# Experts as blocks in program order with a fifth row buffer, and a front that fetches no early rows during the z gates

## The chip, the core and the metric

The kernel runs on one core of one Trainium2 chip. The metric is the device time of one execution in microseconds (us); below is better. The engines are TensorE (PE, its weight loads PEld), VectorE (DVE), ScalarE (ACT), GpSimd (POOL) and SyncE (SP), which issues most of the DMAs. Each engine executes its instructions in the order in which they stand in its queue.

## What is computed

One decoder layer over 1024 tokens of width 1024, all float32, in eight tiles of 128 tokens. First the mixing part (cut here to a line), then product-key retrieval of single-neuron experts ("PEER"), then a last RMSNorm:

```python
x = x + gate_m * (concat(pool_mixer, ssd_mixer(z, x, B, C, dt)) @ w_out)   # after rmsnorm, modulate, h @ w_in
h = modulate(rmsnorm(x, norm_ffn), shift_f, scale_f)
q = (h @ w_query)                      # 8 heads x 2 halves of 128
v1, i1 = top_k(q[:, :, 0] @ keys1, 16); v2, i2 = top_k(q[:, :, 1] @ keys2, 16)
top_s, pos = top_k(v1[..., None] + v2[..., None, :], 16)      # of 16 x 16 pairs
idx, gates = i1 * 128 + i2 at pos, softmax(top_s)             # 128 experts of 16384 for a token
act = gelu(sum_d(h * expert_down[idx]))
x = x + gate_f * sum_k(gates * act * expert_up[idx])
out = rmsnorm(x, norm_final)
```

## The kernel before

**Front.** `front(gi)` (line 390 on) runs three times, over the token tiles 0-1, 2-4 and 5-7. In each: blocks of the input projection with convolution, the SSD chunks, the z gates (`product` with `w_z`, line 522), the output projection (`product` with `w_o`, line 542), the second norm, and the query projection with the scores and the first top 16 (lines 567 to 609). What a tile's experts are is worked out by `select` (line 732). It is a generator: pieces of it are put between the blocks of the next group by `drain(rate)`, with a priority as if they stood 2000 instructions later.

**Two ways for the experts.** Tiles 1 to 4 ("dense", `DT`) go through all 16384 experts on PE: `select` turns their choices into one-hot matmuls and stores a dense gate table `gd` in HBM (lines 812 to 848). Tiles 0, 5, 6, 7 ("gathered", `GT`) fetch the 128 expert rows of each token by indirect DMA on POOL and work on DVE. Tile 0 is done in the front by `ahead` (line 858), two half rows of 4 KB a token in a step, 129 steps; `fetch(n)` takes n of these steps after each block of the front (`FETCH` has n by group, 1.6 in the second and 0.5 in the third). Tiles 5 to 7 are done by `gather` (line 888) beside the dense experts: 128 steps each, a whole row of 8 KB a token (down and up). One step is an indirect DMA into one of four row buffers (three, and one more in the experts' part), a dot product on DVE (line 910), Gelu and gate on ACT (911, 912) and, one step later, the weighted sum on DVE (903), which frees the buffer. Tiles 6 and 7 have their top 16 of scores put off into this part too (`selects`, line 708).

**Dense experts.** `experts` (line 954) goes over 128 blocks of 128 experts. For each: load `raw` (the block's down weights), split it into a rounded part `dnh` (ACT, 1023) and a rest `dnl` (DVE, 1024), 24 matmuls of a faster fp32 format into `m` (1033), Gelu on ACT (1036), times the gates on DVE (1037). For each unit of three blocks, `mm2` (line 993) does 48 matmuls into eight outputs (1007): four stay in PSUM (`res`), four pass through two rotating banks (`rot`) and are added to `ys` in SBUF by DVE (1014). After the last unit each dense tile gets `finish` (line 925).

**What sets the order.** The whole program is laid out at compile time by a scheduler that simulates it and gives each engine the ready instruction of highest priority. The gather steps of the experts' part are drained behind each block (`steps * b // (NK - SB * LEAD)`, line 1042) at the late priority, so where they land between PE's blocks is the scheduler's choice. The memory of the front's pools is used again by the experts' pools; a tile there waits for the last reader of what lay under it.

Of the kernel before, what the change touches and what calls it, by code (L numbers as in the profile page):

```python
# [17 lines left out]
D = 1024  # L18
# [26 lines left out]
LEAD = 2  # L45
# [3 lines left out]
MORE = 1  # L49
# [13 lines left out]
FETCH = (0, 1.6, 0.5)  # L63


class Trunk:
    def __init__(self, ctx, tc, I, out):
        self.ctx, self.tc, self.nc, self.I, self.out = ctx, tc, tc.nc, I, out
        self.bg = []
        self.due, self.owed, self.few = 0, 0, 2  # L70
        self.early, self.taken = None, 0

# [30 lines left out]


    def consts(self):
# [9 lines left out]
        self.rooms = {name: self.pool(name) for name in ("rz", "rx", "rp", "r1")}  # L115
# [182 lines left out]
    def product(self, n, w, kps, a, rate, then=None):  # L298

        for q in range(4):  # L300
            acc = [self.psa.tile([128, 512], FT, name="acc") for _ in range((n + 1) // 2)]
            acc = [acc[i // 2][:, i % 2 * 256:i % 2 * 256 + 256] for i in range(n)]
            for kp in kps:
# [9 lines left out]
                self.fetch(self.frate)  # L313
# [71 lines left out]
    def front(self, gi):  # L385
# [136 lines left out]
        for q, acc in self.product(n, I["w_z"], (0, 1), lambda k, c: h[:, k, c], RATEZ[gi]):  # L522
# [46 lines left out]
        for b in range(16):  # L569
# [33 lines left out]
            for i in range(n):  # L603
# [4 lines left out]
                scr = self.tp.tile([128, 128], FT, name="tscr", bufs=2)  # L608
# [99 lines left out]
    def selects(self, lp):  # L708

        for t, v, pi in self.late:  # L710
            for h in range(0, 8, 2):
                sc = lp.tile([128, 4, 128], FT, name="sc")
                self.nc.sync.dma_start(sc, self.scd[LATE.index(t), :, 2 * h:2 * h + 4])
                for b in range(4):
                    scr = self.tp.tile([128, 128], FT, name="tscr", bufs=2)
                    self.top16(sc[:, b], v[:, h + b // 2, b % 2], pi[:, h + b // 2, b % 2], scr)
                    if b % 2:
                        yield
# [15 lines left out]
    def select(self, t, v, pi):  # L734
# [15 lines left out]
        key = tp.tile([128, 8, 2, 16], BF, name="key")  # L750
        nc.vector.tensor_copy(key, pi)
# [3 lines left out]
        for h in range(8):  # L755
            scr = tp.tile([128, 128], FT, name="tscr", bufs=2)
# [15 lines left out]
        for start, length in ROWS:  # L772
            nc.vector.tensor_scalar(q, p, float(start), float(length - (start == SINGLE)), op0=OP.is_ge, op1=OP.mult)
            nc.vector.tensor_tensor(r2, r2, q, op=OP.subtract)
            if start < SINGLE:
                nc.vector.tensor_scalar(q, p, float(start), None, op0=OP.is_ge)
                nc.vector.tensor_tensor(r1, r1, q, op=OP.add)  # L777
        yield
        idx = tp.tile([128, 2, 8, 16], FT, name="idx")
        for j, r in enumerate((r1, r2)):  # L780
            for h in (0, 4):
# [4 lines left out]
                nc.vector.tensor_tensor(oh, oh, key[:, hs, j].unsqueeze(3).to_broadcast([128, 4, 16, 16]), op=OP.mult)  # L786
# [101 lines left out]
    def gather(self, j):  # L888
# [3 lines left out]
        h2 = gp.tile([128, D], FT, name="h2", bufs=1)  # L892
        nc.sync.dma_start(h2, self.h2r[j * 128:(j + 1) * 128, :])
# [11 lines left out]
        for s in range(128):  # L905
# [9 lines left out]
            prev = (u, a, s)  # L915
            yield
        add(*prev)
# [5 lines left out]
        self.finish(t, [acc[:, :512], acc[:, 512:]], rows, self.residual(xx[:, :D], t), xx[:, D:])  # L923
        yield

# [215 lines left out]
```

## Time and profile before

| | |
|---|---|
| runs | 2895.31, 2899.98, 2903.27 us; median 2899.98 |
| the profiled execution | 2912.44 us, span 2910.6 us, mean granted clock 0.948 |
| busy | PE 91%, DVE 82%, ACT 29%, POOL 30% of the span |
| moved | 893.31 MB, mean 307 GB/s |

The page gives shares of the whole span, which has three parts with different limits: the front (0 to about 1221 us), the dense experts with the gather (to about 2811 us) and what follows PE's last full stretch (to 2910.6 us). A digit in a slice line is a busy share in tenths; PEclk is TensorE's granted clock in tenths of full speed.

### The profile page before, as it was taken

How to read it: one execution, taken by the hardware profiler on the slowest of the kernel's cores; microseconds unless marked ns; L12 is line 12 of the kernel's file. 1: busy time of each engine (PE TensorE's matmuls, PEld its weight loads, DVE VectorE, ACT ScalarE, POOL GpSimd, SP SyncE). 2: the span in 40 equal slices, each digit the busy share in tenths (PEclk: the TensorE clock that was granted, in tenths of full speed). 3: DMA queues.
4: the chain of work that ended last, by engine and by line, in shares of the span. 5: the costliest groups of instructions: out<-in, count | busy, mean ns of one | idle time of the engine just before them, and what ended most of it. 6: DMA issues, size and time to landing. Idle time of an engine off the chain costs nothing. (4 is left out here: it accounts for less than half of the span.)

```text
span 2910.6 us, 31644 instructions
## 1 busy us (share of the span) xinstructions
PE 2663.1 (91%) x10243; PEld 1746.7 (60%) x10244; DVE 2375.6 (82%) x5156; ACT 830.1 (29%) x2244; POOL 884.6 (30%) x679
## 2 busy tenths in 40 slices
PE   8899986789889989699999999999999999999961
PEld 5688555676557876465655666666666666666630
DVE  6625898979999879899999777787877777778887
ACT  3523451322254342322222222222222222222211
POOL 0000066554440005022333333333333333333343
PEclk9999987899989989899999999999999999999985
DMA  8655389999863679888999999899999989998986
GB/s 304 222 172 173 103 296 331 356 362 361 289 234 124 185 220 383 277 310 323 352 354 356 356 366 337 336 364 361 346 348 351 370 320 372 348 368 339 356 320 234
DMA packets 264278, 893.31 MB, mean 307 GB/s; under 512 B 25904, under 2 KB 110000, under 8 KB 212656
## 3 DMA queue, kind: packets, MB, share of 16 engines
q0 software_dynamic: 92448, 541.11, 49.0%
q1 hardware_dynamic: 171664, 350.18, 34.7%
q8 instruction: 81, 1.33, 0.2%
q14 instruction: 85, 0.70, 0.1%
HBM read 840.86 MB, written 50.34 MB: 306 GB/s over the span
## 5 line engine op out<-in xcount | busy, mean ns | idle before, releaser
L907 POOL DMA_INDIRECT row<-in_ud,eidx x384 | 547.5, 1426 | 1105.8 <-DVE yacc L903 870.4
L903 DVE SCALAR_TENSOR_TENSOR yacc<-row,act,yacc 128x1024 f32<-128x1024 f32 x381 | 488.5, 1282 | 67.9 <-ACT act L912 65.1
L910 DVE SCALAR_TENSOR_TENSOR row<-row,h 128x1024 f32<-128x1024 f32 x384 | 467.1, 1218 | 51.1 <-DMA row<-in_ud,eidx 50.8
L1007 PE MATMUL rot<-up,w 128*128 128x512 f32 x1024 | 464.5, 596 | 4.8 <-DVE ys L1014 4.8
L1007 PE MATMUL res<-up,w 128*128 128x512 f32 x1024 | 458.6, 592 | 0.0
L870 POOL DMA_INDIRECT row<-in_ud,eidx x256 | 313.6, 1225 | 417.3 <-DVE rkb L777 102.1
L911 ACT ACTIVATE act<-act 128x1 f32<-128x1 f32 x384 | 77.1, 201 | 976.0 <-DVE row L910 975.6
L1007 PEld LDWEIGHTS rot<-up,w 128*128 128x128 f32 x1024 | 194.9, 191 | 221.8 <-issue 208.3
L1007 PEld LDWEIGHTS res<-up,w 128*128 128x128 f32 x1024 | 193.8, 189 | 200.5 <-issue 189.4
L1033 PE MATMUL m<-h2h,dnh 128*128 128x512 f32 x1024 | 292.9, 427 | 18.9 <-ACT dnh L1023 18.9
L1033 PE MATMUL m<-h2l,dnh 128*128 128x512 f32 x1024 | 285.6, 413 | 0.0
L1033 PE MATMUL m<-h2h,dnl 128*128 128x512 f32 x1024 | 279.6, 412 | 0.0
L1033 PEld LDWEIGHTS m<-h2h,dnh 128*128 128x128 f32 x1024 | 193.5, 189 | 96.8 <-issue 39.5
L307 PE MATMUL acc<-wraw,r 128*128 128x256 f32 x1024 | 239.3, 388 | 8.3 <-ACT s L525 8.3
L435 PE MATMUL acc<-r,wraw 128*128 128x384 f32 (+1 forms) x768 | 235.0, 464 | 2.3 <-ACT s L439 1.3
L581 PE MATMUL acc<-rz,wraw 128*128 128x384 f32 (+1 forms) x768 | 235.3, 457 | 0.0
L1033 PEld LDWEIGHTS m<-h2l,dnh 128*128 128x128 f32 x1024 | 192.6, 188 | 66.5 <-issue 30.4
L1033 PEld LDWEIGHTS m<-h2h,dnl 128*128 128x128 f32 x1024 | 193.4, 189 | 59.2 <-issue 19.1
L307 PEld LDWEIGHTS acc<-wraw,r 128*128 128x128 f32 x1024 | 196.3, 195 | 37.9 <-ACT s L525 9.9
L1014 DVE TENSOR_TENSOR ys<-rot,ys 128x512 f32<-128x512 f32 x168 | 115.4, 687 | 112.1 <-PE rot L1007 111.6
L435 PEld LDWEIGHTS acc<-r,wraw 128*128 128x128 f32 x768 | 147.7, 195 | 81.8 <-issue 8.6
L581 PEld LDWEIGHTS acc<-rz,wraw 128*128 128x128 f32 x768 | 143.7, 194 | 64.0 <-issue 2.3
(298 smaller groups left out, 3271.3 us busy)
## 6 DMA issues: line engine op xcount, KB each, us to landing
up<-in_ud SPq DMA_DIRECT2D x128, 512.0 KB, 7.4
raw<-in_downT SPq DMA_DIRECT2D x128, 512.0 KB, 7.9
gd<-stage SPq DMA_DIRECT2D x32, 1024.0 KB, 9.3
gates<-gd SPq DMA_DIRECT2D x16, 2048.0 KB, 12.3
wraw<-in_w_c SPq DMA_DIRECT2D x48, 512.0 KB, 5.6
wraw<-in_w_q SPq DMA_DIRECT2D x48, 512.0 KB, 6.3
wraw<-in_w_o SPq DMA_DIRECT2D x36, 512.0 KB, 5.2
row<-in_w_ada SPq DMA_DIRECT2D x32, 512.0 KB, 5.3
```

The source lines that it names most:

```text
L307: self.nc.tensor.matmul(acc[i], a(4 * kp + j, slice(i * 128, (i + 1) * 128)), ws[:, j * 256:(j + 1) * 256], start=kp == kps[0] and j == 0 ...
L435: nc.tensor.matmul(acc[:, :T], wc[:, k * 128:(k + 1) * 128], h[:, k], start=k == 0, stop=k == KB - 1)
L581: nc.tensor.matmul(acc[:, :T], wq[:, k * 128:(k + 1) * 128], g[:, k], start=k == 0, stop=k == KB - 1)
L870: nc.gpsimd.indirect_dma_start(out=u[:, i * D:(i + 1) * D], out_offset=None, in_=src, in_offset=bass.IndirectOffsetOnAxis(ap=e[:, s + i:s ...
L903: nc.vector.scalar_tensor_tensor(acc, u[:, D:], a, acc, op0=OP.mult, op1=OP.add)
L907: nc.gpsimd.indirect_dma_start(out=u, out_offset=None, in_=self.I["ud"], in_offset=bass.IndirectOffsetOnAxis(ap=e[:, s:s + 1], axis=0))
L910: nc.vector.scalar_tensor_tensor(u[:, :D], u[:, :D], 1.0, h2, op0=OP.mult, op1=OP.mult, accum_out=a)
L911: nc.scalar.activation(a, a, AF.Gelu)
L1007: nc.tensor.matmul(ps, w[:, ts], up[:, hs], start=st, stop=sp, skip_group_check=True)
L1014: nc.vector.tensor_tensor(ysum[o], ps, ysum[o], op=OP.add)
L1033: nc.tensor.matmul(p1, dn[x][:, k * 128:(k + 1) * 128], h2[y][:, k], start=(k == 0 and n == 0), stop=(k == KB - 1 and n == 2))
```

## The change

1. **Order.** After the early work is drained, everything that `experts` issues on PE, DVE and ACT keeps the order of the program (`in_order` adds an ordering edge between neighbours on an engine). SP and POOL are left to the scheduler.
2. **The loop is written as a pipeline.** `raw` is loaded three blocks ahead, `dnh` made two ahead, `dnl` one ahead; the gates of a block are applied one block later; the 48 matmuls of a unit are spread over the three blocks of the next one; the adds to `ys` come one block later. The gather steps are paced: 384 steps over blocks 4 to 125, at most five a block.
3. **Five row buffers** in place of four (`MORE = 2`); a tile's `h2` is loaded before the tile ahead of it is finished.
4. **Memory.** The experts' pools are put in another order (`raw` first, `ys` and `gates` late; `up` has 6 buffers, not 7, `w` 6, not 4), and the front's rooms too, so that other tiles lie under them.
5. **Late top 16.** Scores come in single loads of 64 KB two ahead, not four at a time; one `tscr` buffer; the steps of it go with the gather of the tile before, one for eight gather steps.
6. **`select`.** The keys are kept twice side by side, so that the product with the one-hots reads pairs; one fused instruction in place of two, seven times.
7. **Front.** `FETCH` is 1.7 and 0.9 in the second and third group, and none is taken during the z gates.

```diff
-LEAD = 2
+FIRST, LAST = 4, 2
+MIX = 8
-MORE = 1
+MORE = 2
-FETCH = (0, 1.6, 0.5)
+FETCH = (0, 1.7, 0.9)
+    def in_order(self, start):
+        last = {}
+        order = mybir.DependencyInfo(mybir.DependencyClass.NoSync, mybir.DependencyReason.DATA)
+        for ins in list(self.nc.cur_bb.bb.instructions)[start:]:
+            if ins.engine in (mybir.EngineType.PE, mybir.EngineType.DVE, mybir.EngineType.Activation):
+                if ins.engine in last:
+                    self.tc.add_manual_dep(ins, last[ins.engine], order, reason="order")
+                last[ins.engine] = ins.name
-        self.rooms = {name: self.pool(name) for name in ("rz", "rx", "rp", "r1")}
+        self.rooms = {name: self.pool(name) for name in ("rx", "rp", "r1", "rz")}
-                self.fetch(self.frate)
+                if then is not False:
+                    self.fetch(self.frate)
...
-        for q, acc in self.product(n, I["w_z"], (0, 1), lambda k, c: h[:, k, c], RATEZ[gi]):
+        for q, acc in self.product(n, I["w_z"], (0, 1), lambda k, c: h[:, k, c], RATEZ[gi], False):
...
-        key = tp.tile([128, 8, 2, 16], BF, name="key")
-        nc.vector.tensor_copy(key, pi)
+        key = tp.tile([128, 2, 8, 16, 2], BF, name="key")
+        nc.vector.tensor_copy(key.rearrange("p j h r d -> p h j r d"), pi.unsqueeze(4).to_broadcast([128, 8, 2, 16, 2]))
...
-                nc.vector.tensor_scalar(q, p, float(start), None, op0=OP.is_ge)
-                nc.vector.tensor_tensor(r1, r1, q, op=OP.add)
+                nc.vector.scalar_tensor_tensor(r1, p, float(start), r1, op0=OP.is_ge, op1=OP.add)
...
-                nc.vector.tensor_tensor(oh, oh, key[:, hs, j].unsqueeze(3).to_broadcast([128, 4, 16, 16]), op=OP.mult)
+                pairs = oh.rearrange("p h r (a b) -> p (h r) a b", b=2)
+                nc.vector.tensor_tensor(pairs, pairs, key[:, j, hs].rearrange("p h r d -> p (h r) d").unsqueeze(2)
+                                        .to_broadcast([128, 64, 8, 2]), op=OP.mult)
...
+        for j in range(EARLY, len(GT)):
+            late = [s for s in self.late if j + 1 < len(GT) and s[0] == GT[j + 1]]
+            self.bg.append(self.mixed(self.gather(j), self.selects(lp, late), MIX))
+        total = 128 * (len(GT) - EARLY)
...
             for j in range(size):
+                want = total * max(b + 1 - FIRST, 0) // (NK - LAST - FIRST) - self.count
+                want = max(min(want, 5), 0)
+                load(b + 3)
...
+                gated(b - 1)
+                if b % GS == 1:
+                    gload(b // GS + 1)
+                steps(min(want, 1))
+                added()
+                if todo:
+                    n = -(-len(todo) // (size - j))
+                    mm2(u - 1, queue, todo[:n])
+                    todo = todo[n:]
+                    if n > 3:
+                        added()
+                steps(min(max(want - 1, 0), 1))
+                low(b + 1)
+                steps(max(want - 2, 0))
+                acts[b] = new("w")
+                nc.scalar.activation(acts[b], p1, AF.Gelu)
+                high(b + 2)
...
+        gated(NK - 1)
+        added()
+        self.in_order(start)
```

Here `high`, `low` and `gated` are the lines 1023, 1024 and 1037 for the block named, `added` is line 1014 (1012 for the first unit), and `steps(n)` takes n steps of the gather.

## Rows read from the trace of the kernel before

**Rows 1.** The page's first two parts: busy time by engine, and the span in 40 slices of 72.8 us (of these, the GB/s that the DMA engines moved).
```profile
PE 2663.1 (91%) x10243; PEld 1746.7 (60%) x10244; DVE 2375.6 (82%) x5156; ACT 830.1 (29%) x2244; POOL 884.6 (30%) x679
...
GB/s 304 222 172 173 103 296 331 356 362 361 289 234 124 185 220 383 277 310 323 352 354 356 356 366 337 336 364 361 346 348 351 370 320 372 348 368 339 356 320 234
```
**Rows 2.** Busy time of each engine in stretches. Columns: the stretch, its length, then PE, PEld, DVE, ACT, POOL busy us (instructions), granted clock, DMA share, GB/s. These are a stretch near the experts' start (with the late top 16 on DVE), their steady part, a single 100 us of it, and the 61 us after PE's last full stretch.
```profile
1300.00:1600.00 300.00, 295.22 (x945) 178.20 (x944) 286.69 (x668) 73.24 (x191) 98.88 (x69) 0.99 0.92 347
1600.00:2700.00 1100.00, 1100.00 (x3554) 669.68 (x3552) 851.08 (x1079) 256.85 (x688) 368.32 (x259) 1.00 0.92 352
2000.00:2100.00 100.00, 100.00 (x323) 60.58 (x322) 78.61 (x98) 23.11 (x62) 33.63 (x24) 1.00 0.92 357
2811.00:2872.00 61.00, 0.00 (x0) 0.00 (x0) 46.59 (x58) 9.44 (x38) 29.48 (x19) 0.53 0.88 328
```
**Rows 3.** PE's instructions in order of time at the end (start, us, line, tiles, count, idle before and its releaser).
```profile
2807.80 2.74 PE L1007 MATMUL rot<-up,w 128*128 128x512 f32 x6
2881.54 2.07 PE L1002 MATMUL rot<-ys,ident 128*128 128x512 f32 x2 [71.00 <-DVE dnl L932]
...
2888.24 2.74 PE L1007 MATMUL rot<-up,w 128*128 128x512 f32 x6
```
**Rows 4.** POOL's instructions in order of time in the same stretch: a row fetch, and the fourth one after it, which is the last of all.
```profile
2857.07 1.68 POOL L907 DMA_INDIRECT row<-in_ud,eidx  x1 [1.24 <-DVE yacc L903]
...
2870.08 1.68 POOL L907 DMA_INDIRECT row<-in_ud,eidx  x1 [1.24 <-DVE yacc L903]
```
**Rows 5.** PE at the start of the experts.
```profile
1221.35 3.78 PE L1033 MATMUL m<-h2h,dnh 128*128 128x512 f32 x8 [18.94 <-ACT dnh L1023]
...
1235.86 0.59 PE L1007 MATMUL res<-up,w 128*128 128x512 f32 x1
```
**Rows 6.** SP's DMA issues at the same place, and DVE's first product with the gates.
```profile
1205.81 0.62 SPq L848 DMA_DIRECT2D gd<-stage  x1
1210.81 4.10 SPq L942 DMA_DIRECT2D out<-row  x2
1214.96 0.45 SPq L1021 DMA_DIRECT2D raw<-in_downT  x1
1217.92 0.33 SPq L1027 DMA_DIRECT2D gates<-gd  x1
...
1230.57 0.69 DVE L1037 TENSOR_TENSOR w<-w,gates 128x512 f32<-128x512 f32 x1 [0.70 <-ACT w L1036]
```
**Rows 7.** PE in the steady part: the first matmuls of a block, three blocks apart, and eight of the 24 matmuls between others of their kind.
```profile
2208.14 2.42 PE L1033 MATMUL m<-h2h,dnh 128*128 128x512 f32 x8
...
2222.84 1.98 PE L1033 MATMUL m<-h2l,dnh 128*128 128x512 f32 x8
2224.65 1.88 PE L1007 MATMUL res<-up,w 128*128 128x512 f32 x4
...
2245.19 2.40 PE L1033 MATMUL m<-h2h,dnh 128*128 128x512 f32 x8
```
**Rows 8.** The page's groups of instructions: busy us, mean ns of one, idle of the engine before them and what ended most of it.
```profile
L907 POOL DMA_INDIRECT row<-in_ud,eidx x384 | 547.5, 1426 | 1105.8 <-DVE yacc L903 870.4
L903 DVE SCALAR_TENSOR_TENSOR yacc<-row,act,yacc 128x1024 f32<-128x1024 f32 x381 | 488.5, 1282 | 67.9 <-ACT act L912 65.1
L910 DVE SCALAR_TENSOR_TENSOR row<-row,h 128x1024 f32<-128x1024 f32 x384 | 467.1, 1218 | 51.1 <-DMA row<-in_ud,eidx 50.8
```
**Rows 9.** Waits in the experts' part (who waits for whom: us in total, times, longest).
```profile
DVE yacc L903 <- ACT act L912: 65.1, 109, 0.6
DVE row L910 <- DMA row<-in_ud,eidx: 50.8, 32, 3.8
```
**Rows 10.** DMA issues by line: KB each, median us from issue to landing.
```profile
up<-in_ud SPq DMA_DIRECT2D x128, 512.0 KB, 7.4
raw<-in_downT SPq DMA_DIRECT2D x128, 512.0 KB, 7.9
gd<-stage SPq DMA_DIRECT2D x32, 1024.0 KB, 9.3
gates<-gd SPq DMA_DIRECT2D x16, 2048.0 KB, 12.3
```
**Rows 11.** Stretches of the front, columns as in rows 2: the z gates of the second group, its output projection, the z gates of the third group, and the third group's query projection.
```profile
436.00:526.00 90.00, 66.66 (x278) 52.47 (x277) 80.26 (x151) 17.40 (x51) 57.43 (x46) 0.83 0.92 332
575.00:632.00 57.00, 52.09 (x301) 45.34 (x298) 44.79 (x88) 13.15 (x37) 28.16 (x23) 1.00 1.04 390
908.00:957.00 49.00, 47.79 (x268) 41.32 (x267) 46.50 (x147) 19.16 (x51) 0.00 (x0) 1.00 0.36 108
1090.00:1198.00 108.00, 101.89 (x561) 69.82 (x560) 100.33 (x217) 31.09 (x63) 41.24 (x31) 0.96 0.90 321
```
**Rows 12.** Groups of DVE instructions over the whole span, shapes apart: the product with the keys, an instruction of the same size that reads pairs, the copy of the keys, and the two that are fused.
```profile
L786 DVE TENSOR_TENSOR oh<-oh,key 128x1024 bf16<-128x1024 bf16 x32 | 39.0, 1219 | 0.3
...
L826 DVE TENSOR_TENSOR hota<-keyno,etr 128x1024 f16<-128x1024 f16 x64 | 43.6, 685 | 22.6 <-PE g L843 20.7 <-ACT etr L808 1.7
...
L751 DVE CAST key<-pi 128x256 bf16<-128x256 uint32 x8 | 2.3, 282 | 0.0
...
L777 DVE TENSOR_TENSOR rkb<-rkb,rkd 128x128 bf16<-128x128 bf16 x56 | 12.2, 219 | 0.8
L776 DVE TENSOR_SCALAR rkd<-rka 128x128 bf16<-128x128 bf16 x56 | 10.9, 195 | 0.8
```

More of the change, by code (lines that the diff above doesn't have):

```diff
@@ L981, in experts @@
         self.wk = self.pool("fin", side="right")
-        lp = self.pool("late", 2, reuse_waits="tile")
-        self.bg += [self.early, self.mixed(self.gather(EARLY), self.selects(lp), 3)]
-        self.bg += [self.gather(j) for j in range(EARLY + 1, len(GT))]
-        steps = 129 * len(GT) - self.taken + 40
-        gates = None
-        done = 0
-        queue = []
+        lp = self.pool("late", 3, reuse_waits="tile")
+        self.bg.append(self.early)
+        self.drain()
+        start = len(nc.cur_bb.bb.instructions)
+        for j in range(EARLY, len(GT)):
+            late = [s for s in self.late if j + 1 < len(GT) and s[0] == GT[j + 1]]
+            self.bg.append(self.mixed(self.gather(j), self.selects(lp, late), MIX))
+        total = 128 * (len(GT) - EARLY)
         units = [1] + [SB] * ((NK - SB - 2) // SB) + [1, SB]
@@ L991, in experts, with mm2 @@
         last = len(units) - 1
-        def mm2(u, ws, some=outs):
+        order = [o for pair in zip(outs[4:], outs[:4]) for o in pair]
+        sums = dict(held)
+        adds = []
+        def mm2(u, ws, some):
             for o in some:
@@ L1010, in mm2, with added, load, gload @@
                 elif o in ysum:
[L1011 to L1014 removed]
+                    adds.append((u, o, ps))
+        def added():
+            while adds:
+                u, o, ps = adds.pop(0)
+                if u == 0:
+                    nc.vector.tensor_copy(ysum[o], ps)
+                else:
+                    nc.vector.tensor_tensor(ysum[o], ps, ysum[o], op=OP.add)
+        raws, highs, lows, ups, acts, gates = {}, {}, {}, {}, {}, {}
+        def load(b):
+            if b < NK:
+                raws[b] = new("raw")
+                nc.sync.dma_start(raws[b], I["downT"][b])
+        def gload(g):
+            if g < NK // GS:
+                gates[g] = new("gates")
+                nc.sync.dma_start(gates[g], self.gd[g])
+        def high(b):
+            if b < NK:
+                highs[b] = new("dnh")
+                nc.scalar.activation(highs[b], raws[b], AF.Copy)
+        def low(b):
+            if b < NK:
+                lows[b] = new("dnl")
+                nc.vector.tensor_tensor(lows[b], raws.pop(b), highs[b].bitcast(FT), op=OP.subtract)
+        def gated(b):
+            if b >= 0:
+                w = acts[b].rearrange("p (c t) -> p c t", t=TC)
+                nc.vector.tensor_tensor(w, w, gates[b // GS][:, :, b % GS], op=OP.mult)
+        def steps(n):
+            end = self.count + n
+            for _ in range(n + 1):
+                if self.count < end:
+                    self.drain(1)
+        for b in range(3):
+            load(b)
+        gload(0)
+        high(0)
+        high(1)
+        low(0)
+        queue = None
         b = 0
```

106 lines of the change are left out of this document (52 added, 54 removed).

## The prediction

> **What bounds the kernel now.** I read the page's shares, then busy time in stretches, then PE's order of time at the two seams, then the groups and waits of the experts' part. PE is busy 91% of the span [rows 1], but that is a mean. In the 1100 us in the middle of the experts PE is busy without a gap at full clock, while DVE has 77% and DMA 0.92 [rows 2]: there PE alone sets the pace. Then PE stops: its last full stretch ends at 2807.80 + 2.74 = 2810.5, and it waits 71.00 us, up to 2881.5 [rows 3]. What runs in that hole is the rest of the gather: POOL's last row fetch starts at 2870.08, one every 3.25 us ((2870.08 - 2857.07) / 4) [rows 4], so some 21 of the 384 rows come after PE has run dry. So the end is set by PE (to 2810.5), then by rows that had been put too late, then by `finish`.
>
> Were those rows late because the hardware could not fetch faster? No: DVE waited for a row to land only 32 times, 50.8 us in all [rows 9], while POOL waited 870.4 us for DVE to free a buffer [rows 8], and DVE was idle 23% of the time [rows 2]. The order in the queues had 24 fetches in 100 us [rows 2], and nothing asked for more.
>
> **The change part by part.**
>
> *The tail.* PE's work in the experts stays: 1024 x 3 matmuls of the fast format and 2048 others. From 1221.35 to 2810.5 PE took 1589.2 us [rows 3, 5]; the 12 + 4 matmuls done after the hole, 16 x 0.43 = 6.9 us, make 1596. (Three blocks take 2245.19 - 2208.14 = 37.05 us; a matmul of the fast format takes (2224.65 - 2222.84) / 8 = 0.227, 72 of them 16.3, which leaves 0.43 for each of the 48 others [rows 7].) At 12.35 us a block 128 blocks are 1581, so 15 us of the 1596 are the slow start and small waits. I keep 1596. In the new order all 384 steps stand before block 126, so the 71 us hole cannot stand behind PE's work any more. If the rows don't keep up, PE waits for them instead, through `dnl` and the gates that stand behind the steps in DVE's queue. That is the term to size.
>
> *Can the rows keep up?* New pace: 384 rows over 122 blocks, 3.15 a block of 12.35 us, 25.5 in 100 us against 24.
> DVE: 78.6 us of 100 now [rows 2]; 1.5 rows more at 1.22 + 1.28 = 2.5 us [rows 8] add 3.8; the late top 16 of two tiles now lies ahead of this stretch: DVE has 286.69 us in the 300 before it, where the steady 77.4% would be 232 [rows 2], so I estimate 65 us with what comes before 1300, and spread over 122 blocks (1507 us) it adds 4.3. Sum 87%, or 10.7 of 12.35 us: room of 1.65 us a block.
> DMA: a block moves 2 x 0.524 MB (`raw`, `up`), 2.097 / 8 = 0.262 MB of gates [rows 10] and 3.15 x 1.049 MB of rows (128 x 2048 x 4 bytes): 4.61 MB. At a share of 0.92 the engines moved 357 GB/s [rows 2], so 388 at a full one: 11.9 us a block, 96% of PE's time. This is the tight one.
> Buffers: four of them turned over in 4 x 4.17 = 16.7 us each in steady state, and in 4 x 3.25 = 13.0 us alone [rows 2, 4]. Five at 12.35 / 3.15 = 3.92 us a row give 19.6 us each, 2.9 us more than now, for a fuller DMA and for waits in the fixed order.
> Price: zero if all fits; the bounds are 0 and, if the mean rate cannot pass 357 GB/s, (4.61 MB / 357 GB/s = 12.91) - 12.35 = 0.56 us, times 122, 69 us. Since a stretch at 390 GB/s and slices at 383 and 372 stand in this trace [rows 1, 11], I take a tenth of a microsecond a block: +12 us.
> One rule of the Trainium skill speaks against this ("DMA: Bandwidth & Descriptors", section "Bandwidth"): for transfers from HBM the limit is the core's share of HBM, about 358 GB/s. By it a block would take 4.61 / 358 = 12.88 us and the sum below would be 53 us higher; the 383 to 390 GB/s above, on a single core, speak against it.
>
> *The start.* PE stands 18.94 us before its first expert matmul, for `dnh`, for `raw`, whose load is issued at 1214.96 behind stores of the front [rows 5, 6]. With `raw` over early-freed memory this wait can go. What is late next is the gates: the last piece of the gate table is stored at 1205.81, the load of the first gates follows at 1217.92, and they are applied at 1230.57 [rows 6]; the store lands in 9.3 us and the load in 12.3 [rows 10], so 1205.8 + 9.3 + 12.3 is 1227 at best. PE can do the first matmuls of blocks 0 and 1 ahead of that (2 x 5.4 us, three times 1.81 for eight [rows 7]), but its third piece of work, `mm2` of block 0, cannot start before about 1231.3, where it started at 1235.86, with three matmuls of block 2 done [rows 5]. So the start gains 4 us, not 19; bounds 0 and 19. I take -4.
>
> *The front.* The stretch of the z gates takes 90 us in the second group, with early rows on DVE, the DMA at 0.92 and a granted clock of 0.83, and 49 us in the third, without them [rows 11]. At most 41 us go there. The 13 steps (8 calls x 1.6) go elsewhere: the third group now takes 0.9 x 44 = 40 steps in place of 0.5 x 52 = 26, and 14 steps are 28 half rows at about 1.28 us of DVE [rows 8] (a dot or a weighted sum over a half row has the same shape), 36 us, in a group whose query projection has DVE busy 100 of 108 us [rows 11]. `select` gets cheaper: four products of 1219 ns become about 685 (an instruction of that size that reads pairs) [rows 12], -2.14; seven pairs of 219 + 195 become single ones of about 219, -1.37; a key copy twice as long, +0.28: 3.2 us a tile, six tiles in the front, 19 us. Early rows are fillers that the scheduler also pulls ahead of their place, so neither the 41 nor the 36 will come whole. Bounds -60 and +36; I take -10, about half of the 19 that is sure.
>
> *After PE.* From PE's last matmul (2890.98) to the end it is 19.6 us, with the finish of the last gathered tile and of three dense ones piled up [rows 3]. The gathered tile is now finished under blocks 126 and 127; what stays is a chain of one dense tile behind the others. I take 16, bounds 12 and 20.
>
> *At nothing:* 24 more score loads of 64 KB on SP (24 x 0.33 us over 1507 us, as the load of the gates [rows 6]); `raw`, queued behind them, is loaded three blocks, 37 us, ahead and lands in 7.9 [rows 10], and without that room each late load would be PE's wait. One `tscr` buffer instead of two: DVE writes and reads it in its own order. Fewer `up` buffers: a load still comes a block or more, 12 us, ahead of its use and lands in 7.4 [rows 10]. The gathered tiles' last adds move from POOL to DVE, 6 x 0.7 us in DVE's room. The new ordering adds waits: behind a row that has not landed stand, in DVE's queue, `dnl` of the next block, the adds and the gates, and for these PE waits; the cover is the 1.65 us a block, and beyond it every microsecond is PE's.
>
> *Sum.* 1221.35 - 10 - 4 + 1596 + 12 + 16 = 2831.4 us of span, against 2910.6: -79.2 us. The profiled execution (2912.44) lies 12.5 us above the median of the runs (2899.98), so the difference is taken from the median: 2820.8.
>
> **The rivals.**
>
> A. *The DMA is full.* The mean rate stays at 357 GB/s, and the hole turns into 0.56 us of PE idle in each block, 69 us in place of 12: 2878. For it: 0.92 share in steady state and 337 to 357 GB/s in every stretch of it; against it: nothing waited for rows to land [rows 9]. The Trainium skill's 358 GB/s, as cited, would give 2874.
>
> B. *Slower: the fixed order ties PE to single rows.* A DVE that stands for a row or for ACT has no other work to turn to. Now such a wait is 1.6 us (50.8 / 32) for a row and up to 0.6 for ACT [rows 8, 9]. With 10.7 us of work, waits of 1.65 us a block are free; from 1.65 + 0.75 = 2.4 us a block on the whole gain (91 us with the 12) is eaten, 122 x 0.75. One row wait and two of ACT, 2.8 us, make blocks of 13.5 us, 122 x 1.15 = 140 us in place of 12: 2949. For it: three engines that must be ready within 13% of one another, in an order that cannot bend. Against it: five buffers, and fetches that run ahead of DVE.
>
> C. *The front takes all it is offered:* -60 in place of -10, PE's waits 5 in place of 12: 2764. Against it: what the second group sheds the third one carries.
>
> D. *The front loses:* the 36 us of moved rows stand on DVE's path: 2867.
>
> **Chances.** Forecast 0.58, A 0.15, B 0.09, C 0.12, D 0.06. The forecast's own range is 2790 to 2852 (front and start +-15, rows 0 to 25, the end +-4). The range to hold the time 8 times in 10 goes from C to just above A: 2762 to 2885. A measurement of this kernel tells changes of over about 0.3% from none, here 8.7 us. Faster: the forecast, C, D and two thirds of A, 0.86; same: the upper third of A, 0.05; slower: B, 0.09.
>
> **What would show it.** Right: PE's wait for `dnl` before the last four pairs of matmuls gone; the last row fetch before PE's last block; 25 fetches in 100 us, at 365 to 375 GB/s; three blocks of PE in 37 to 37.5 us; z gates of the second group under 60 us; `oh<-oh,key` near 685 ns; the first `mm2` still behind the gates. A would show as DVE waits for rows and a block of 12.8 to 12.9 us at no more than 360 GB/s; B as PE waiting for `dnl` or the gates in every block with the DMA below 0.92, perhaps with a lower granted clock. The forecast is wrong if PE's experts take more than 1640 us or the front ends later than 1221.

## The result, and the profile after

The changed kernel takes 2880.02 us (median; 2878.38 to 2883.49), the kernel before 2899.98 (2895.31 to 2905.25): a ratio of 0.9931, 95% interval 0.9913 to 0.9949. It is faster by 0.7%, 20 us, where 79 were forecast. The profiled execution took 2879.54 us, span 2877.8, so here the profile and the median agree, while the profiled execution before lay 12.5 us above its median. In spans, forecast 2831.4 stands against 2877.8.

First the page: busy time by engine, GB/s in the 40 slices, and the three groups of the gather (compare [rows 1, 8]).

```profile
PE 2651.4 (92%) x10244; PEld 1731.5 (60%) x10244; DVE 2366.2 (82%) x5106; ACT 833.3 (29%) x2247; POOL 804.2 (28%) x673
...
GB/s 307 207 185 167 101 303 325 362 358 371 308 302 110 178 206 217 245 299 363 378 388 385 369 358 308 384 403 381 392 360 362 377 348 415 371 390 356 361 291 124
...
L936 POOL DMA_INDIRECT row<-in_ud,eidx x384 | 479.2, 1248 | 1023.1 <-DVE yacc L932 967.9
L939 DVE SCALAR_TENSOR_TENSOR row<-row,h 128x1024 f32<-128x1024 f32 x384 | 469.8, 1224 | 78.9 <-DMA row<-in_ud,eidx 78.4
L932 DVE SCALAR_TENSOR_TENSOR yacc<-row,act,yacc 128x1024 f32<-128x1024 f32 x381 | 487.9, 1281 | 0.0
```

Line 936 is the row fetch (907 before), 939 its dot product (910), 932 its weighted sum (903). Next, busy time in stretches of the experts, columns as in rows 2; the last four answer to [rows 2].

```profile
1200.00:1300.00 100.00, 45.58 (x152) 28.65 (x150) 78.88 (x133) 12.00 (x24) 40.29 (x35) 0.72 0.82 306
1300.00:1600.00 300.00, 300.00 (x967) 182.39 (x966) 271.14 (x470) 74.83 (x205) 95.78 (x77) 1.00 0.96 380
1600.00:2700.00 1100.00, 1084.14 (x3491) 659.68 (x3489) 952.70 (x1508) 272.44 (x740) 343.07 (x277) 0.99 0.94 373
2000.00:2100.00 100.00, 100.00 (x324) 60.62 (x322) 88.50 (x147) 24.49 (x68) 31.95 (x26) 1.00 0.98 391
2811.00:2872.00 61.00, 48.82 (x142) 26.98 (x140) 41.92 (x94) 13.22 (x36) 8.10 (x8) 0.95 0.32 122
```

The tail hole is gone: where PE stood for 61 us it now works for 49. In the steady part PE is full, with 26 fetches in 100 us and DVE at 88%. Two places are bad: the first 100 us of the experts, in which PE is busy 46 us, and 16 us missing between 1600 and 2700. Here is PE at the start, in order of time.

```profile
1180.21 2.11 PE L1121 MATMUL m<-h2h,dnh 128*128 128x512 f32 x8 [0.46 <-ACT dnh L1081]
...
1219.99 2.05 PE L1052 MATMUL rot<-up,w 128*128 128x512 f32 x2 [18.47 <-issue]
...
1247.90 2.74 PE L1052 MATMUL res<-up,w 128*128 128x512 f32 x6
1278.35 4.61 PE L1052 MATMUL rot<-up,w 128*128 128x512 f32 x6 [27.71 <-DVE ys L1062]
...
1299.25 4.40 PE L1052 MATMUL rot<-up,w 128*128 128x512 f32 x6 [8.23 <-DVE ys L1064]
...
1305.66 2.40 PE L1121 MATMUL m<-h2h,dnh 128*128 128x512 f32 x8
```

The first expert matmul comes 41 us sooner than before (1221.35, [rows 5]), the first `mm2` at 1219.99, behind the gates as forecast. But then PE stands 27.71 us, and block 6, whose first matmul is the last line, starts at 1305.66, 85.7 us after that `mm2`. In the kernel before, PE went through this stretch without a wait, 46.1 us from 1235.86 [rows 5] to block 6:

```profile
1281.99 0.63 PE L1033 MATMUL m<-h2h,dnh 128*128 128x512 f32 x2
```

From block 6 on most blocks of the changed kernel keep the forecast pace (three in 37.07 us). DVE at the same place shows what PE waited for: one line is 25 instructions.

```profile
1219.20 0.69 DVE L1091 TENSOR_TENSOR w<-w,gates 128x512 f32<-128x512 f32 x1 [7.01 <-DMA gates<-gd]
...
1239.56 32.98 DVE L902 SCALAR_TENSOR_TENSOR yacc<-row,acts,yacc 128x1024 f32<-128x1024 f32 x25
1272.57 1.29 DVE L969 TENSOR_TENSOR row<-yacc,row 128x512 f32<-128x512 f32 x2
...
1277.62 0.68 DVE L1062 COPY ys<-rot 128x512 f32<-128x512 f32 x1
...
1296.16 1.23 DVE L939 SCALAR_TENSOR_TENSOR row<-row,h 128x1024 f32<-128x1024 f32 x1 [9.07 <-DMA row<-in_ud,eidx]
```

Line 902 is the weighted sum of `ahead`: tile 0's early rows, followed by its finish (969). The copy that frees a `rot` bank for PE stands behind all of them. On POOL one sees why so many early rows were still to be done.

```profile
893.86 0.58 POOL L1017 DMA_DIRECT2D h2h<-h2td  x1 [30.54 <-ACT tok L675]
1041.25 0.55 POOL L1017 DMA_DIRECT2D h2l<-h2td  x1 [146.81 <-PE g L866]
1187.20 0.17 POOL L354 MEMSET sums<- 128x4 f32 x3 [145.41 <-ACT w L1138]
1201.80 1.03 POOL L893 DMA_INDIRECT row<-in_ud,eidx  x1 [14.43 <-PE g L866]
```

Between 862 and 1201.8 POOL fetched no row. What stood ahead in its queue, two loads of the dense tiles' input (`h2h`, `h2l`), the memsets and then the fetch itself, waited for instructions of the front; I read these waits as memory that the front still held. Before, 32 half rows were fetched between 1078 and 1151, all inside the front; now the last 24 come between 1201.8 and 1261.8.

### The profile page after: what moved, and what is told of

Read it like the earlier page. It is cut to its first block, busy times and chain, and to the rows that moved or that the text cites. A ratio compares the mean times of both kernels' runs of the same rounds, so it can differ in the third digit from the quotient of the medians.

```text
span 2877.8 us, 31441 instructions
## 1 busy us (share of the span) xinstructions
PE 2651.4 (92%) x10244; PEld 1731.5 (60%) x10244; DVE 2366.2 (82%) x5106; ACT 833.3 (29%) x2247; POOL 804.2 (28%) x673
## 4 chain that ended last, share of the span: by engine, by line
PE 68%; DVE 15%; DMA 7%; issue 6%; POOL 3%; ACT 2%; SPq 0%; POOLq 0%; DVEq 0%; ACTq 0%
PE m L1121 22%; PE rot L1052 14%; PE res L1052 14%; PE acc L320 6%; PE acc L595 5%; PE acc L449 3%; DMA row<-in_ud,eidx 3%; POOL row L893 2%; DVE row L898 2%; DVE yacc L902 1%; PE g L866 1%; DMA row<-in_w_ada 1%; DVE s L484 1%; DVE tscr L717 1%; PE ss L611 1%
## 5 line engine op out<-in xcount | busy, mean ns | idle before, releaser
L936 POOL DMA_INDIRECT row<-in_ud,eidx x384 | 479.2, 1248 | 1023.1 <-DVE yacc L932 967.9
L1052 PE MATMUL rot<-up,w 128*128 128x512 f32 x1024 | 476.2, 600 | 64.3 <-DVE ys L1062 27.7
L1052 PE MATMUL res<-up,w 128*128 128x512 f32 x1024 | 470.4, 594 | 1.4 <-DVE w L1091 1.4
L893 POOL DMA_INDIRECT row<-in_ud,eidx x256 | 312.3, 1220 | 364.8 <-PE tr L667 99.2
L1121 PE MATMUL m<-h2h,dnh 128*128 128x512 f32 x1024 | 310.0, 445 | 0.5 <-ACT dnh L1081 0.5
L1121 PE MATMUL m<-h2h,dnl 128*128 128x512 f32 x1024 | 255.5, 392 | 8.7 <-DVE dnl L1086 8.7
L1121 PE MATMUL m<-h2l,dnh 128*128 128x512 f32 x1024 | 253.7, 390 | 0.0
L320 PE MATMUL acc<-wraw,r 128*128 128x256 f32 x1024 | 233.4, 381 | 0.0
```

What stands on the lines that cost most here:

```text
L320: self.nc.tensor.matmul(acc[i], a(4 * kp + j, slice(i * 128, (i + 1) * 128)), ws[:, j * 256:(j + 1) * 256], start=kp == kps[0] and j == 0 ...
L893: nc.gpsimd.indirect_dma_start(out=u[:, i * D:(i + 1) * D], out_offset=None, in_=src, in_offset=bass.IndirectOffsetOnAxis(ap=e[:, s + i:s ...
L936: nc.gpsimd.indirect_dma_start(out=u, out_offset=None, in_=self.I["ud"], in_offset=bass.IndirectOffsetOnAxis(ap=e[:, s:s + 1], axis=0))
L1052: nc.tensor.matmul(ps, w[:, ts], up[:, hs], start=st, stop=sp, skip_group_check=True)
L1121: nc.tensor.matmul(p1, x[b][:, k * 128:(k + 1) * 128], h2[y][:, k], start=(k == 0 and n == 0), stop=(k == KB - 1 and n == 2))
```

## The experiments

All times are medians beside runs of the kernel before; ratios are to that kernel, and the changed kernel's is 0.9931. "Block 6" is PE's first matmul of the seventh block of 128 experts.

### The start

**Without the left-over rows.** In `ahead`, a flag that is set when the experts begin skips the steps still to be done: 18 steps, 36 half rows, which are left out of tile 0's sum. 24 of them are those that came after 1201.8, the other 12 had come before.

```diff
                 for s in range(0, 128, 2):
+                    if self.cut:
+                        continue
```


> The changed kernel without the early steps that are left over when the experts begin: 36 of the 128 experts of each token of tile 0 are not added (its finish stays). This prices them. Theory 1: 36 x 1.28 = 46 us of DVE go, 31 of them from the hole at the start, so block 6 comes at 1262 to 1275 and the time is 2832 to 2848 us. Rival (the gate table alone sets the start): block 6 not before 1295, 2865 to 2880 us.

2840.56 us, ratio 0.9788 (0.9772 to 0.9805); block 6 at 1270.6, 35 us sooner. So the left-over rows cost 40 us, as theory 1 had it, and the gate table alone does not set the start. The first `mm2` came at 1225.1, so its stretch to block 6 is 45.5 us, as in the kernel before:

```profile
1270.63 2.42 PE L1124 MATMUL m<-h2h,dnh 128*128 128x512 f32 x8
```

**Three buffers for them.** The two added buffers join the rotation after the early steps.

```diff
-        self.rows += range(ROWBUFS, ROWBUFS + MORE)
         self.few = 3
...
         self.drain()
+        self.rows += range(ROWBUFS, ROWBUFS + MORE)
```


> The changed kernel, but the early steps of tile 0 that are left when the experts begin rotate through three row buffers; the two added ones join only after them. Theory 1 (the leftover rows start the experts late because two of five buffers lie on memory that the front's last one-hots still read, so POOL stands until 1201.8 us): the 24 half rows go to before 1180, the hole of 27.7 us at 1250 and the 8.2 us behind it vanish. From the first mm2 at 1220, PE's work up to block 6 is four blocks' 24 fast matmuls (4 x 5.45) and 40 others (40 x 0.43), 39 us, so block 6 starts at about 1260 to 1270 where the changed kernel has it at 1305.7: 2835 to 2845 us. Rival (the gates and DVE's load set the start, whichever row buffers are used): block 6 not before 1295, 2868 to 2882 us.

2872.78 us, 0.9898 (0.9881 to 0.9915). The rows did go into the front, up to 936 us, and the wait of 27.7 us went. But the first expert matmul slid from 1180.2 to 1205.3, the first `mm2` from 1220.0 to 1257.5, and block 6 came at 1303.1. The rival's numbers hold: moved, and only some 7 us saved.

**Three buffers, behind `h2l`.** As above, and from the seventh of these steps on an ordering edge on POOL puts the row fetches behind the load of `h2l`.

```diff
+        for i in [i for i in pool if i.name not in ahead][12:]:
+            self.tc.add_manual_dep(i, last.name, order, reason="order")
```


> The changed kernel with the left over early steps on three row buffers, and on POOL all but the first six of them behind the load of h2l, so that they come after about 1041 us. Three buffers alone brought them to 900 to 936 us, where DVE is 95% busy, and the front ended 25 us later. From 1000 to 1200 DVE of the changed kernel is busy 132 of 200 us. Theory 1 (the rows are free only where DVE has room): 24 half rows (31 us) go there, the front ends within 8 us of 1180, block 6 comes at 1262 to 1275 in place of 1305.7: 2838 to 2850 us. Rival (they delay the one-hots of the last dense tile wherever they go, and with these the gate table and the first mm2): block 6 not before 1290, 2865 to 2880 us.

2866.08 us, 0.9876 (0.986 to 0.9893), block 6 at 1293.2. Better by some 16 us, yet outside theory 1: 24 half rows between 1054 and 1138 put the first expert matmul from 1180.2 to 1209.6, 29 us, as much as their 24 x 1.28 = 31 us of DVE. This tells what the 41 us were that the front had seemed to gain: most of it was these rows, taken out of it. Why DVE, which in the changed kernel idles 52 of the 139 us from 1041 to 1180, could not take them for less was not settled.

**Paced with the gather.** The early steps left over stand at the head of the paced steps, inside the fixed order. (Tile 0's last adds move from POOL to DVE with them.)

```diff
-        self.bg.append(self.early)
         self.drain()
         start = len(nc.cur_bb.bb.instructions)
+        self.bg.append(self.early)
+        self.count = 0
...
-        total = 128 * (len(GT) - EARLY)
+        total = 128 * (len(GT) - EARLY) + 128 - self.taken
```


> The changed kernel, but the 18 early steps of tile 0 that are left over, and tile 0's finish, are not issued in one lump ahead of the blocks: they stand at the head of the paced steps (402 over blocks 4 to 125 in place of 384), inside the fixed order. Without those steps block 6 began at 1270.6 in place of 1305.7 and the time was 39 us under the changed kernel's. Theory 1 (what costs is the lump that stands ahead of the blocks in DVE's and ACT's queues, not the work): block 6 at 1265 to 1280, and 18 x 2.56 = 46 us of DVE and 3.30 rows a block find room beside PE, so 2842 to 2856 us. Rival (DVE and the DMA owe this work and have no room left at 3.3 rows a block): the blocks get longer than 12.36 us and the time is 2865 to 2885 us.

2853.04 us, 0.9827 (0.9809 to 0.9845): the fastest complete kernel of the study, 1.7% under the kernel before and 1.0% under the changed one. Block 6 comes 45.6 us after the first `mm2`. The same work, spread, gives back 30 of the 40 us: the stretch at the start is whole again, but the first `mm2` comes 7 us later and the long blocks at the tile changes (see there) hold 31 us in place of 22. Its first `mm2`, its block 6 and two stretches, columns as above:

```profile
1227.42 2.04 PE L1054 MATMUL rot<-up,w 128*128 128x512 f32 x2 [21.71 <-issue]
...
1273.01 2.42 PE L1123 MATMUL m<-h2h,dnh 128*128 128x512 f32 x8
...
1400.00:1700.00 300.00, 300.00 (x974) 183.26 (x973) 278.76 (x481) 76.67 (x213) 101.98 (x82) 1.00 0.99 394
1850.00:2250.00 400.00, 400.00 (x1294) 243.72 (x1293) 372.97 (x651) 103.54 (x286) 139.78 (x108) 1.00 0.98 391
```

PE is full with DVE at 93% and the DMA at 0.98 to 0.99, so 3.3 rows a block still fit between the tile changes.

**The front's old pace.**

```diff
-FETCH = (0, 1.7, 0.9)
+FETCH = (0, 1.6, 0.5)
...
-        ... RATEZ[gi], False):
+        ... RATEZ[gi]):
```


> The changed kernel with the front's pace of early rows as it was (1.6 and 0.5, z gates included), all else as changed. Theory 1: the same blocked row buffers, and some 16 steps left over in place of 12, so 4 x 2 x 1.28 = 10 us more at the start, and the second group's z gates long again while the third group sheds its share: 2882 to 2905 us. Rival D of the prediction (moving rows into the third group loses in the front): 2845 to 2872 us.

2888.37 us, 0.9954 (0.9938 to 0.9971): theory 1. 32 half rows are left over in place of 24, 8 x 1.28 = 10 us; block 6 comes at 1313.4, 7.7 us later. The first expert matmul stays at 1178.8: the new pace did not shorten the front.

### The fixed order, the fifth buffer and the memory

**No order.** The call of `in_order` is taken out.

```diff
-        self.in_order(start)
```


> The changed kernel without the ordering edges: PE, DVE and ACT in the experts' part go where the scheduler puts them. Theory 1 (the order costs only at the start and at tile changes, where a late row holds everything behind it): the scheduler puts the same instructions nearly in the same places, 2865 to 2895 us, and a hole before PE's end can come back. Rival B of the prediction (the fixed order ties PE to single rows all along): faster by over 30 us, below 2850.

2924.67 us, 1.0083 (1.0066 to 1.0099): slower than every number expected. No block was long at the tile changes, and block 9 started at 1284, 59 us before the changed kernel's. But the rows fell behind, 20 to 25 in 100 us (23 in the mean from 1300 to 2700, where the changed kernel has 25), and PE paid at its end:

```profile
2897.88 2.08 PE L1047 MATMUL rot<-ys,ident 128*128 128x512 f32 x2 [121.02 <-DVE dnl L969]
```

So the order is worth 44 us net, and without it the hole comes back; rival B of the prediction falls.

**Order from block 8 on.**

```diff
             for j in range(size):
+                if b == 8:
+                    start = len(nc.cur_bb.bb.instructions)
```


> The changed kernel with the ordering edges from block 8 on; the first eight blocks are left to the scheduler. With no edges at all, block 9 began at 1284 us where the changed kernel has it at 1343, but the rows fell behind and PE stood 121 us before its end. Theory 1 (at the start the fixed order costs, later it gains): the start of the one and the rest of the other, 35 to 55 us less: 2825 to 2845 us. Rival (DVE owes the same work in any order, and what PE gains at the start it waits for later): 2865 to 2882 us.

2886.51 us, 0.9943 (0.9926 to 0.9961). PE ran through the first eight blocks early and then stood 59.8 us for one add to `ys`; block 9 came at 1350.7, later than in the fixed order (1342.7). DVE owes the same work in any order, and PE's lead was waited for: the rival's account, at a time a little above its range.

**Four buffers.**

```diff
-MORE = 2
+MORE = 1
```


> The changed kernel with four row buffers in place of five. Theory (the fifth buffer is what lets rows come every 3.9 us beside PE in the fixed order): four turned over in 16.7 us each before, so 4.17 us a row, and a block of 3.15 rows needs 13.1 us: 122 x 0.78 = 95 us more, 2950 to 2980 us. Rival (the buffers turn over faster in the fixed order, since a row's two DVE passes stand closer): 2880 to 2920 us.

2948.55 us, 1.0156 (1.0138 to 1.0173). The wait of DVE for rows (line 939) between 1300 and 2800:

```profile
DVE row L939 <- DMA row<-in_ud,eidx: 228.6, 141, 8.2
```

With five buffers it is

```profile
DVE row L939 <- DMA row<-in_ud,eidx: 69.0, 46, 10.1
```

The theory's account, at a time just under its range. Without its fifth buffer the change is slower than the kernel before.

**The old order of the pools.** `more` first, `raw` late, the front's rooms as before.

```diff
-        self.rooms = {name: self.pool(name) for name in ("rx", "rp", "r1", "rz")}
+        self.rooms = {name: self.pool(name) for name in ("rz", "rx", "rp", "r1")}
...
+        self.more = self.pool("more", reuse_waits="tile")
+        kinds = {"ys": ..., "up": ..., "gates": ..., "h2h": ..., "h2l": ..., "raw": ..., "dnh": ..., "dnl": ..., "w": ...}
```


> The changed kernel with part 4 undone: the experts' pools and the front's rooms in their old order (the added row buffers first, raw late), the buffer counts as changed. If the place of the two added row buffers were all that holds the left over rows, 24 half rows would come before 1170 us as in the kernel before, and the time would be that of the rows held behind h2l, 2860 to 2870 us. The other theory: the memsets of the finish tiles' sums stand on POOL between those rows and wait for the last of the front's memory (to about 1187 us) wherever the buffers lie, so most of the rows still come after that, and PE waits for raw as before (up to 19 us): 2875 to 2895 us.

2873.4 us, 0.9917 (0.9897 to 0.9937). 23 of 24 half rows still came after 1170, as the other theory said, but not for the memsets. POOL stood ahead of them, at the first fetch into the second added buffer:

```profile
1177.97 0.94 POOL L893 DMA_INDIRECT row<-in_ud,eidx  x1 [103.88 <-ACT sc L616]
```

One fetch, into the first added buffer, came at 1072.67. So with two more buffers in the rotation at least one lies under late memory in either layout, and the fetches behind it wait in line. PE waited 27.6 us for `raw` here, which the new layout had removed; all the same the kernel is no slower, and its time lies between the two ranges: the gain of the new layout is not shown.

### The tile changes

In the changed kernel one block near 1800 takes 26.4 us in place of 13.2, one near 2310 19.9, and two others 2.0 more together: 21.9 us. POOL at the first change:

```profile
1769.64 1.68 POOL L936 DMA_INDIRECT row<-in_ud,eidx  x1 [2.00 <-DVE yacc L932]
1794.92 0.10 POOL L354 MEMSET sums<- 128x4 f32 x1 [23.61 <-DVE rs_h L295]
1798.64 0.95 POOL L936 DMA_INDIRECT row<-in_ud,eidx  x1 [3.62 <-DVE eidx L817]
...
1812.45 0.94 POOL L936 DMA_INDIRECT row<-in_ud,eidx  x1 [9.14 <-DMA out<-row]
```

For 29 us no row is fetched: the next tile's list (`eidx`) is ready only at 1798. The fifth buffer comes later still, when the finished tile's output has landed.

**Late top 16 sooner.**

```diff
-MIX = 8
+MIX = 4
```


> The changed kernel, but one step of the late top 16 goes with four gather steps, not eight, so that the next tile's list of rows is ready long before the tile changes. Theory 1 (at a tile change nothing can be fetched until select has written the list, and in the fixed order everything on DVE stands behind the first row that lands): the long blocks near 1800 (26.4 us in place of 13.2) and near 2320 (19.9) shrink to the common pitch, 15 to 21 us less: 2859 to 2865 us. Rival (the finish of the old tile, its rows and its norm, makes the stall): the long blocks stay, 2876 to 2884 us. A third way: more DVE work at the start of each tile makes waits there, and the gain is half.

2882.25 us, 0.9936 (0.9915 to 0.9957): no gain. The long blocks shrank to 20.3 and 14.4, but two new ones, 19.2 and 19.7, stood where 5.4 us of `select` lie in one piece, ahead of the gates in one and of an add to `ys` in the other, so neither theory had it all.

**In smaller pieces.** One late step for five, and `select` of the late tiles yields more often.

```diff
-MIX = 8
+MIX = 5
...
+                if h == 4 or t in LATE:
+                    yield
```


> The changed kernel with one late step for five gather steps, and the late tiles' select cut into smaller steps (its product with the one-hots in pieces of 2.7 us of DVE in place of 5.4, its ranks in three pieces). With one step for four and the steps as they were, the block at the tile change went from 26.4 to 20.3 us and the next from 19.9 to 14.4, but two new long blocks (19.2 and 19.7) stood where 5.4 us of select stand in one piece ahead of the gates. Theory 1 (both the missing list and the length of one piece make the stalls): no block over 15 us but the one at the first tile change, 15 to 20 us less than the changed kernel: 2860 to 2866 us. Rival (what stalls is the sum of DVE's work around the tile change): the time stays, 2874 to 2884 us.

2873.18 us, 0.9908 (0.989 to 0.9927). The second long block is gone, no new one came, the first stays at 25.9: 7 us of the 22. DVE stands at the first for a row:

```profile
1818.91 1.23 DVE L942 SCALAR_TENSOR_TENSOR row<-row,h 128x1024 f32<-128x1024 f32 x1 [15.83 <-DMA row<-in_ud,eidx]
```

The data for the output was ready at 1793.1, but SP, which had stood 16.5 us behind a load of `up` that waited for its buffer, issued the store at 1800.8; by the program, two of the five buffers were out of use until it landed.

```profile
1799.47 1.19 SPq L1120 DMA_DIRECT2D up<-in_ud  x2
1800.76 0.38 SPq L983 DMA_DIRECT2D out<-row  x1
```

**Output through POOL's queue.**

```diff
-            nc.sync.dma_start(self.out[t * 128:(t + 1) * 128, hs], x[:, hs])
+            (nc.gpsimd if t in GT else nc.sync).dma_start(self.out[t * 128:(t + 1) * 128, hs], x[:, hs])
```


> The finer select with one step for five, and the gathered tiles' output stored through POOL's queue instead of SP's. There the block at the first tile change was still 25.9 us, and DVE stood 15.8 us for a row that POOL fetched only when a store of the finished tile had landed; that store was issued 8 us after its data, behind loads of up that waited on SP for a buffer. Theory (SP's queue, in order, holds two of five row buffers): the wait shrinks to below 8 us and the block to below 19 us: 6 to 11 us less than with the finer select alone, 2862 to 2868 us. Rival (two of five buffers are gone for the finish whatever queue stores them): the block stays above 22 us, 2870 to 2876 us.

2866.57 us, 0.9882 (0.9865 to 0.99): the time that the theory gave, though the block only went to 22.8, as the rival had it, and DVE still stood 11.2 us for the row. Of the 7 us gained only 3 lie at this block, so the time was in part luck. SP's queue is part of the stall; what keeps the rest is open.

### Together

**The three repairs.** The paced steps, the finer select and the output through POOL's queue.

```diff
-MIX = 8
+MIX = 5
...
+        self.bg.append(self.early)
+        self.count = 0
...
+            (nc.gpsimd if t in GT else nc.sync).dma_start(self.out[t * 128:(t + 1) * 128, hs], x[:, hs])
```


> The changed kernel with the three edits together: left over early steps paced with the gather, the finer select with one step for five, the gathered tiles' output through POOL's queue. Theory: the gains add, 25 to 38 us from the start and 12 to 20 us from the tile changes: 2825 to 2848 us. Rival (with 3.3 rows a block the rows become the pace, and what is won at the tile changes is waited for later): 2850 to 2870 us.

2855.73 us, 0.9841 (0.9824 to 0.9857): the rival's time. The gains do not add.

**Two of them.** As above, with the output through SP's queue again.

```diff
-            (nc.gpsimd if t in GT else nc.sync).dma_start(self.out[t * 128:(t + 1) * 128, hs], x[:, hs])
+            nc.sync.dma_start(self.out[t * 128:(t + 1) * 128, hs], x[:, hs])
```


> The left over early steps paced with the gather, and the finer select with one step for five; the gathered tiles' output through SP's queue again. All three together took 2855.7 us, no less than the paced steps alone (2853.0). Theory 1 (at 3.3 rows a block the rows are the pace, so what a shorter select gives is waited for elsewhere): 2846 to 2858 us, and PE's long blocks stay at the tile changes. Rival (the output through POOL's queue delays the row fetches and eats the gain of the finer select): 2836 to 2846 us.

2859.28 us, 0.986 (0.9843 to 0.9876). This is just above theory 1's range. With paced rows the finer select gains nothing, and the long blocks sit at the tile changes again (23.1, 26.1, 27.1 us), so POOL's queue is not what ate the gain. DVE waits longer for rows between 1300 and 2800, with the finer select (second line) than without it (first):

```profile
DVE row L940 <- DMA row<-in_ud,eidx: 67.3, 53, 12.9
DVE row L943 <- DMA row<-in_ud,eidx: 87.2, 53, 16.8
```

But the rows are not the pace all along, as theory 1 had it: away from the tile changes three blocks take 37.07 us in both kernels. What is lost is lost at the tile changes; which of DVE's work and the buffers' turnover sets it there was not tried.

## Why the prediction was wrong

The direction and the account of the tail were right; the size was wrong because of the start. In spans the sum was 1207.35 + 1608 + 16; measured are 1180.2 to the first expert matmul, 1683.6 to PE's end (2863.8) and 14.0 after: -27.1, +75.6, -2.0, together +46.4. This split misleads, because the first matmul came sooner and the first `mm2`, which stands behind the gates, did not. From the first `mm2` it reads: 1.3 us early there (1219.99, forecast 1231.3 - 10); 39.6 lost from there to block 6 (85.7 against 46.1 before, which the forecast left as it was); 10.2 lost from block 6 to PE's end, where 21.9 at the tile changes stand against the 12 that were forecast; 2.0 gained after. The other 12.5 us of the 59 are the profiled execution of before, which was that much slower than its median, while the one of after is not.

**The tail: right.** The last row fetch stands ahead of PE's last block, which starts at 2832.5, and no hole is left. (Of the rows that came late before, the trace has 19 fetches after 2810.5, not 21.)

```profile
2814.56 1.14 POOL L936 DMA_INDIRECT row<-in_ud,eidx  x1 [1.80 <-DVE yacc L932]
```

**Can the rows keep up: right, with its price as a size.** I took 12 us. The steady blocks cost nothing: DVE was forecast at 87% and is at 88.5. What is paid, 21.9 us, is paid at the tile changes, which the step did not look at: it spread `select` over all blocks as a mean, but it comes in pieces, and a list of rows that is not ready stops all fetches.

**The start: this step failed.** It said "So the start gains 4 us, not 19", from the gates alone, and the sum kept 15 us for "the slow start and small waits". The gates came as it said, 11 us earlier (1219.20 against 1230.57, [rows 6]), and the first `mm2` with them. But the step took the early rows as the front's affair, and did not ask where those go that the front leaves over. The drain ahead of the fixed order put them between the front and the blocks, in DVE's queue ahead of the copy that frees a bank for PE. From the first `mm2` to block 6 PE's work is four blocks' 24 fast matmuls at 0.227 and 52 others at 0.43, 44 us; the stretch took 46.1 before, 85.7 in the changed kernel, 45.5 without the left-over rows and 45.6 with them paced. So the term that was missing is 40 us. The run without these rows, whose first `mm2` came 5 us later, is 36 us shorter in its profiled span and 40 us faster in its median.

**The front: a gain of another kind.** "I take -10" was about half of what `select` was to give; the first expert matmul came 41 us sooner. By the run behind `h2l`, which has 24 half rows in the front and the rest as changed, 29 of these are the rows that left (1209.6 to 1180.2), and 12 are the change's own. Those 12 are less than the wait for `raw` that went, 18.94 us [rows 5]: with the rows in it the front itself ran some 6 us longer, not shorter. Both of the step's own terms were off. The z gates: I set 90 us for them [rows 11], but that stretch held more than the gates. By ACT's Silu of the group (instructions, min/median/max ns, first and last start) they took 48 us before:

```profile
L525 ACT ACTIVATE s<-acc x12: 365/384/385, 476.3 to 524.5; 128x256 f32<-128x256 f32 x12
```

and 52 in the changed kernel:

```profile
L539 ACT ACTIVATE s<-acc x12: 365/384/385, 483.6 to 535.9; 128x256 f32<-128x256 f32 x12
```

so there were no 41 us to gain. "Under 60 us" came true, and said nothing. And of the moved rows the last 24 halves, 31 us of DVE, stood behind the front and not in it.

**`select`:** the product is 686 ns, as read from the row of its size [rows 12]; the fused instruction takes 283, not 219. No run takes this part back alone, so what it gives in time is not shown.

```profile
L808 DVE TENSOR_TENSOR oh<-oh,key 128x1024 bf16<-128x1024 bf16 x32 | 21.9, 686 | 0.4
L798 DVE SCALAR_TENSOR_TENSOR rkb<-rka,rkb 128x128 bf16<-128x128 bf16 x56 | 15.9, 283 | 0.0
```

**The rivals.** A fell: 373 to 391 GB/s at a share of 0.94 to 0.98. That its 2878 is nearly the measured time is luck. (Its "337 to 357 GB/s in every stretch" of the kernel before was too narrow, too: the steady slices of [rows 1] go from 320 to 372.) The Trainium skill ("DMA: Bandwidth & Descriptors", section "Bandwidth") lets HBM's share of about 358 GB/s bind, and the trace does not agree; another page of the Trainium skill ("Perfetto Trace Analysis", section "Roofline") says that a core alone can pass that share, up to some 120% of it, and with this the 391 agree. B fell with the run without the order: the fixed order loses at the start and at tile changes, and gains far more at the end. C and D both missed that the rows leave the front without being done. The mark set for a wrong forecast, over 1640 us for PE's experts, was the right one: 1683.6.

## What to carry to other kernels

Where background work is drained "before" a part that is then put in a fixed order, count what is left of it at that point: it becomes a lump at the head of every in-order queue. Paced into the order at a few microseconds a block, the same work gave back 30 of its 40 us. A front that ends sooner is no gain until one has found which work left it. A deeper ring of buffers helps from when all of them are free: here the fifth was worth 68 us, but a buffer under late memory held up the fetches into all the others, since the queue takes them in turn. And work that a mean rate hides is to be looked at in its pieces, and at the places where one item ends and the next needs its list.

## What the runs showed of the hardware

Beside a full PE the DMA engines moved 394 GB/s over 300 us at a share of 0.99 (the paced run), and 541 of the kernel's 893 MB came through POOL's queue; rival A had 357.

A short wait of PE cost more than its length: after 27.71 and 8.23 us the next six matmuls of the slower format took 4.61 and 4.40 us in place of 2.74. The granted clock from 1200 to 1300 was 0.72 in the mean; from 1262 to 1282, in PE's long wait and the first matmuls behind it, it was 0.50, the lower of its two levels (1.2 GHz).

A queue that nobody watched set a buffer's life: on SP a store of 0.4 us stood 8 us behind loads that waited for buffers.
